# The rows of cumulated step logarithms spread over the partitions by DMA from DRAM, where selector matmuls spread them

## The chip, the cores and the metric

One core of a Trainium2 chip runs the whole program. Five engines work side by side: TensorE (PE, with PEld for its weight loads), VectorE (DVE), ScalarE (ACT), GpSimd (POOL) and SyncE (SP), which here issues most DMAs. Each engine executes its own instructions in the order in which they stand in its queue, and an instruction that must wait for another engine or for a DMA holds up all that stand behind it. The metric is the device time of one execution in microseconds (us). Below, a wide matmul is one of 512 columns with rounded 4-byte operands (lines 141 to 143).

## What is computed

A trunk of two layers over 512 tokens of width 1024. Each layer adds three branches to the stream (differential attention, latent attention, a state-space scan), then a gated feed-forward part. The change lies in the scan. Its core in the reference:

```python
da = (dt * a)                       # 512 tokens x 16 heads, in 4 chunks of 128 tokens
cs = jnp.cumsum(da, axis=2)         # within a chunk
seg = cs[:, :, :, None] - cs[:, :, None, :]
decay = jnp.exp(jnp.where(causal, seg, -jnp.inf))
cb = jnp.einsum('bclgn,bcsgn->bclsg', cm, bm)
y_diag = jnp.einsum('bclsgr,bcsgrp->bclgrp', cb[..., None] * decay, xdt)
```

For each head the kernel needs a matrix exp(min(cs[l], cs[s]) - cs[s]) with s on the partitions and l along the row. So the head's row cs[0..511] has to stand on all 128 partitions.

## The kernel before

Activations lie transposed, features on partitions and the 512 tokens along the row. A product with a weight matrix is taken in three passes, since each operand is split into a rounded part and a rest (hh and hl, wh and wl): `mm3`, lines 140 to 143, for products whose result has features on partitions (`lin_feat`), and lines 220 to 222 for those with tokens on partitions (`lin_tok`). Weights come in pieces of 512 KB by SyncE (tile wr, three buffers); ScalarE makes wh (line 132), VectorE wl (line 133), which frees wr. Products collect in PSUM banks: a pool `mb` of four for the products and a pool `ab` of four for all else.

The scan (in `mix`) runs over four groups of four heads. For group g it takes in text order: two products for x (`lin_feat`, evacuated by `ev_x`: a convolution on ScalarE and VectorE, tile u, lines 873 to 880), the tail of the group before, two products for B and C (`ev_bc`), in the first group `decays`, a product for z (`lin_tok`, evacuated by `ev_z`, tile sz, lines 901 and 902), transposes (lines 910, 922), the products of C and B (line 927, masked into cb, line 929), x scaled by dt (xdt, line 914) and by the decay to the chunk's end (xte, line 934), chunk states (matmuls of line 940, prev, lines 942 to 947), then for each of its four heads r:

- line 953: a matmul whose stationary operand is a column of sel spread over 128 columns, and whose moving operand is cs_r. Rows 0 to 15 of cs_r hold the 16 rounded rows, rows 32 to 47 the rests, all others zero, so the head's row appears on all partitions of a PSUM bank, `ab`;
- line 955: VectorE takes the minimum with the head's column, into tile dec (three buffers);
- line 958: ScalarE, four exponentials in place; line 959: VectorE, dec times cb;
- line 961: eight records of matmuls, dec against xdt, into two banks; after them dec's buffer is free.

Then y collects the two banks (line 964), the read-out of the states (matmuls of line 967, yo and y, lines 969 and 972) and the gate (line 973), its squares go through ScalarE (line 977), the power is taken on GpSimd (line 110, tile yn_r), VectorE scales y (line 982), and the group's tail transposes it on TensorE (line 986) and splits it (lines 989 and 990).

The order of the instructions on each engine isn't written out by hand in this stage: a scheduler lays it out when the program is built, by its own estimates, and mixes the next group's products in between. The buffers of a tile go round in turn, so head n has the dec buffer of head n-3. GpSimd has no DMAs in this stage before the change.

Of the kernel before, what the change touches and what calls it, by code (L numbers as in the profile page):

```python
# [9 lines left out]
F32 = mybir.dt.float32  # L10
F32R = mybir.dt.float32r
I32 = mybir.dt.int32
AF = mybir.ActivationFunctionType
ALU = mybir.AluOpType
# [4 lines left out]
P = 128  # L19
S = 512  # L20
T = S // P
# [8 lines left out]
SSM_H, SSM_G, SSM_HD = 16, 4, 64  # L30
# [35 lines left out]
def trunk_kernel(ctx: ExitStack, tc: tile.TileContext, a: dict, out: bass.AP):  # L66
    nc = tc.nc

    cst = ctx.enter_context(tc.tile_pool(name="cst", bufs=1, reuse_waits="tile"))
# [12 lines left out]
    dram = ctx.enter_context(tc.tile_pool(name="dram", bufs=1, space=DRAM))  # L82
# [4 lines left out]
    def abank():  # L87
        return banks["a"].tile([P, 512], F32, name="ab")
# [5 lines left out]
    ident = cst.tile([P, P], F32, name="ident")  # L94
# [5 lines left out]
    nhalf = cst.tile([P, 1], F32, name="nhalf")  # L100
    nc.vector.memset(nhalf, -0.5)

    sel = cst.tile([P, SSM_H], F32R, name="sel")
    nc.vector.tensor_copy(out=sel, in_=ident[:, 0:SSM_H])
    nc.vector.tensor_copy(out=sel[32:48], in_=ident[0:SSM_H, 0:SSM_H])
    def rstd_of(ss, n, width, name):
        ms = small([P, n], name + "_ms")
        nc.vector.tensor_scalar(out=ms, in0=ss, scalar1=1.0 / width, scalar2=EPS, op0=ALU.mult, op1=ALU.add)
# [464 lines left out]

    bias_d = dram.tile([DA_H, P, BLK[T]], F32, name="bias_d")
    x_d = dram.tile([P, KT, S], F32, name="x_d")
    QG = P // BUCKETS
    NJ = P // (DA_H * QG)
    NSIGN = 5
    early, ahead, SLOW, DEEP = [], [0], (6,), 1
    ORDER = (7, 4, 0, 5, 1, 2, 3, 6)  # L580

    W = 2 * P + QG

# [158 lines left out]
    def mix(l, x, hh, hl, ckr, cq, latp, scope):  # L742
# [93 lines left out]
        nc.vector.scalar_tensor_tensor(out=dt, in0=dt, scalar=0.0, in1=poly, op0=ALU.max, op1=ALU.add)  # L836
        da = ssd.tile([P, T, SSM_H], F32, name="da")
        nc.vector.tensor_tensor(out=da, in0=dt, in1=rv["a"].unsqueeze(1).broadcast_to([P, T, SSM_H]), op=ALU.mult)
        zeros = ssd.tile([P, S], F32, name="cb")
        nc.vector.memset(zeros, 0.0)  # L840
        cs_r = ssd.tile([P, S], F32R, name="cs_r")
        nc.vector.tensor_copy(out=cs_r, in_=zeros)
        cs, ncs, tot, ecs, te = (ssd.tile([P, T, SSM_H], F32, name=nm) for nm in ("cs", "ncs", "tot", "ecs", "te"))

        def decays():

            cp = abank()
            daf = da.rearrange("p t h -> p (t h)")
            nc.tensor.matmul(cp[:, 0:n16], tri, daf, start=True, stop=True)
            nc.tensor.matmul(cp[:, n16:2 * n16], ones, daf, start=True, stop=True)  # L850
            ct = abank()
            for c in range(T):
                nc.tensor.matmul(ct[0:SSM_H, c * P:(c + 1) * P], da[:, c], tri, start=True, stop=True)
            nc.scalar.activation(cs_r[0:SSM_H], ct[0:SSM_H], AF.Copy)
            nc.vector.tensor_tensor(out=cs_r[32:32 + SSM_H], in0=ct[0:SSM_H], in1=cs_r[0:SSM_H], op=ALU.subtract)
            flat = "p t h -> p (t h)"
            nc.vector.tensor_copy(out=cs.rearrange(flat), in_=cp[:, 0:n16])
            nc.vector.tensor_scalar(out=ncs.rearrange(flat), in0=cp[:, 0:n16], scalar1=-1.0, scalar2=None, op0=ALU.mult)
            nc.scalar.activation(ecs.rearrange(flat), cp[:, 0:n16], AF.Exp)
            nc.vector.tensor_tensor(out=te.rearrange(flat), in0=ncs.rearrange(flat), in1=cp[:, n16:2 * n16], op=ALU.add)  # L860
            nc.scalar.activation(te, te, AF.Exp)
            nc.scalar.activation(tot.rearrange(flat), cp[:, n16:2 * n16], AF.Exp)
# [3 lines left out]
        with ssd_scope:  # L866
            tails = []
            for g in range(SSM_G):
# [38 lines left out]
                for i in range(2):  # L907
                    tp = abank()
                    for c in range(T):
# [5 lines left out]
                                            in1=dt[:, :, hs].unsqueeze(3).broadcast_to([P, T, 2, SSM_HD]), op=ALU.mult)  # L915
                    nc.vector.tensor_tensor(out=y[:, :, sl].rearrange("p c (r d) -> p c r d", r=2), in0=tv,
                                            in1=rv["dvec"][:, hs].unsqueeze(1).unsqueeze(3).broadcast_to([P, T, 2, SSM_HD]),
                                            op=ALU.mult)
# [6 lines left out]
                for c in range(T):  # L925
                    cs_ = slice(c * P, (c + 1) * P)
                    nc.tensor.matmul(cbp[:, cs_], bmT[:, cs_], cmT[:, cs_], start=True, stop=True)
                cb = sp.tile([P, S], F32, name="cb")
                nc.vector.tensor_tensor(out=cb.rearrange("p (c l) -> p c l", c=T), in0=cbp.rearrange("p (c l) -> p c l", c=T),
                                        in1=tri.unsqueeze(1).broadcast_to([P, T, P]), op=ALU.mult)  # L930

                xte = sp.tile([P, T - 1, 256], F32, name="xte")
                for c in range(T - 1):
                    nc.vector.tensor_tensor(out=xte[:, c].rearrange("p (r d) -> p r d", r=4),
                                            in0=xdt[:, c].rearrange("p (r d) -> p r d", r=4),
# [13 lines left out]
                yps = [abank().rearrange("p (c d) -> p c d", c=2) for _ in range(2)]  # L949
                for r in range(4):  # L950
                    h = 4 * g + r
                    lp_ = abank()
                    nc.tensor.matmul(lp_, sel[:, h:h + 1].broadcast_to([P, P]), cs_r, start=True, stop=True)
                    dec = sp.tile([P, T, P], F32, name="dec", bufs=3)
                    nc.vector.tensor_tensor(out=dec, in0=lp_.rearrange("p (c l) -> p c l", c=T),
                                            in1=cs[:, :, h:h + 1].broadcast_to([P, T, P]), op=ALU.min)
                    for c in range(T):
                        nc.scalar.activation(dec[:, c], dec[:, c], AF.Exp, bias=ncs[:, c, h:h + 1])
                    nc.vector.tensor_tensor(out=dec, in0=dec, in1=cb.rearrange("p (c d) -> p c d", c=T), op=ALU.mult)
                    for c in range(T):  # L960
                        nc.tensor.matmul(yps[c // 2][:, c % 2, r * SSM_HD:(r + 1) * SSM_HD], dec[:, c],  # L961
                                         xdt[:, c, r * SSM_HD:(r + 1) * SSM_HD], start=True, stop=True)
# [618 lines left out]
```

## Time and profile before

| | |
|---|---|
| median of 3 runs | 2087.01 us (2086.53 to 2087.76) |
| the profiled execution | 2087.19 us |
| its span in the trace | 2085.2 us |
| instructions in the trace | 30158 |
| moved by DMA | 237.20 MB, a mean of 114 GB/s |
| of it by SyncE's queue | 232.63 MB |
| of it by GpSimd's queue | 2.65 MB |

Span and execution differ by 2.0 us at the program's ends. The scan of the first layer lies between 84 and 300 us of the span, that of the second between 1095 and 1310 us. PE is counted busy while a matmul is under way, and the ends of matmuls are modelled, so a busy PE need not be a PE at its peak; idle time on another engine costs nothing while PE has work.

### The profile page before, as it was taken

To read this page: it belongs to the slowest core of one execution; us is meant where nothing else is said; L and a number is where in the kernel's file an instruction comes from. 1 tells how busy PE (TensorE), PEld (TensorE's weight loads), DVE (VectorE), ACT (ScalarE), POOL (GpSimd) and SP (SyncE) were. 2 spreads that over 40 slices of the span, in tenths; PEclk is the share of its full clock that TensorE was granted. 3 is DMA by queue.
4 is the path that set the end of the run, shared out by engine and by line. 5 is a ranking of instruction groups with operands and counts; after the bars stand their busy time and mean duration, and the time that the engine had idled before them with its cause. 6 is when DMAs were issued, how large, how long until landed. Compare 5 with 4: busy or idle time off the path is not lost.

```text
span 2085.2 us, 30158 instructions
## 1 busy us (share of the span) xinstructions
PE 2060.7 (99%) x11469; PEld 1794.4 (86%) x11469; DVE 1415.1 (68%) x2731; ACT 923.4 (44%) x1702; POOL 136.0 (7%) x162
## 2 busy tenths in 40 slices
PE   8999999999999999999999999999999999999999
PEld 7889988899888988888898888889998888888888
DVE  7788887747876778657767887765566566553553
ACT  6744445535533444224344544454444334432431
POOL 4200011002100000000000000110020000000000
PEclk8999999999999999999999999999999999999999
DMA  8523232243455265655443222212333242323322
GB/s 268 154 61 92 71 117 86 86 123 105 143 157 171 85 189 171 193 175 159 156 136 91 71 61 88 64 48 79 95 89 93 91 132 91 101 91 96 97 91 81
DMA packets 224542, 237.20 MB, mean 114 GB/s; under 512 B 16126, under 2 KB 195742, under 8 KB 224142
## 3 DMA queue, kind: packets, MB, share of 16 engines
q1 hardware_dynamic: 221646, 232.63, 36.5%
q0 software_dynamic: 2752, 2.65, 0.5%
q8 instruction: 90, 1.47, 0.3%
q14 instruction: 54, 0.44, 0.1%
HBM read 226.30 MB, written 8.91 MB: 113 GB/s over the span
## 4 chain that ended last, share of the span: by engine, by line
PE 85%; DVE 5%; issue 5%; DMA 2%; POOL 1%; ACT 1%; SPq 0%; POOLq 0%; DVEq 0%; ACTq 0%
PE mb L141 20%; PE mb L142 20%; PE mb L143 20%; PE mb L220 3%; PE mb L222 3%; PE mb L221 3%; PE ab L1168 2%; PE mb L662 1%; PE ab L1136 1%; DMA wg<-in_ada_w_dram 1%; DVE wl L133 1%; PE ab L961 1%; DVE macc L518 1%; PE ab L1319 1%; PE ab L1078 1%
## 5 line engine op out<-in xcount | busy, mean ns | idle before, releaser
L141 PE MATMUL mb<-hh,wh 128*128 128x512 f32 (+1 forms) x1376 | 538.5, 392 | 2.9 <-DVE modsum L530 1.4
L143 PE MATMUL mb<-hh,wl 128*128 128x512 f32 (+1 forms) x1376 | 532.9, 387 | 0.0
L142 PE MATMUL mb<-hl,wh 128*128 128x512 f32 (+1 forms) x1376 | 532.5, 387 | 0.0
L133 DVE TENSOR_TENSOR wl<-wr,wh 128x1024 fp32r<-128x1024 f32 (+2 forms) x312 | 375.2, 1204 | 201.2 <-ACT wh L132 195.5
L132 ACT ACTIVATE wh<-wr 128x1024 fp32r<-128x1024 f32 (+2 forms) x312 | 324.5, 1041 | 337.3 <-PE mb L142 257.4
L141 PEld LDWEIGHTS mb<-hh,wh 128*128 128x128 f32 x1376 | 258.6, 188 | 53.4 <-DVE modsum L530 2.6
L143 PEld LDWEIGHTS mb<-hh,wl 128*128 128x128 f32 x1376 | 258.7, 188 | 51.4
L142 PEld LDWEIGHTS mb<-hl,wh 128*128 128x128 f32 x1376 | 259.0, 188 | 49.0 <-DVE hl L698 1.2
L1416 DVE SCALAR_TENSOR_TENSOR fu<-mb,vec,fu 128x510 f32<-128x510 f32 (+1 forms) x176 | 129.9, 746 | 91.2 <-ACT fu L1414 89.6
L220 PE MATMUL mb<-wh,hh 128*128 128x256 f32 x640 | 182.4, 285 | 0.0
L221 PE MATMUL mb<-wl,hh 128*128 128x256 f32 x640 | 181.2, 283 | 0.0
L222 PE MATMUL mb<-wh,hl 128*128 128x256 f32 x640 | 181.2, 283 | 0.0
L141 PE MATMUL mb<-gh,wh 128*128 128x512 f32 (+1 forms) x432 | 152.3, 353 | 0.0
L143 PE MATMUL mb<-gh,wl 128*128 128x512 f32 (+1 forms) x432 | 151.7, 351 | 0.0
L142 PE MATMUL mb<-gl,wh 128*128 128x512 f32 (+1 forms) x432 | 151.7, 351 | 0.0
L1414 ACT ACTIVATE fu<-mb,vec 128x512 f32<-128x512 f32 x88 | 67.7, 772 | 149.0 <-PE mb L143 149.0
L220 PEld LDWEIGHTS mb<-wh,hh 128*128 128x128 f32 x640 | 122.6, 192 | 0.8 <-ACT wh L132 0.4
L221 PEld LDWEIGHTS mb<-wl,hh 128*128 128x128 f32 x640 | 122.6, 192 | 0.4
L222 PEld LDWEIGHTS mb<-wh,hl 128*128 128x128 f32 x640 | 122.6, 192 | 0.0
L518 DVE SCALAR_TENSOR_TENSOR macc<-wg,c_act,macc 128x512 f32<-128x512 f32 x140 | 104.8, 749 | 22.9 <-DMA wg<-in_ada_w_dram 22.3
L141 PE MATMUL mb<-yh,wh 128*128 128x512 f32 x256 | 105.4, 412 | 0.9 <-ACT g L765 0.9
L142 PE MATMUL mb<-yl,wh 128*128 128x512 f32 x256 | 101.2, 395 | 0.0
(334 smaller groups left out, 3427.4 us busy)
## 6 DMA issues: line engine op xcount, KB each, us to landing
wr<-in_w_in_dram SPq DMA_DIRECT2D x88, 512.0 KB
wr<-in_ffn_w_up_dram SPq DMA_DIRECT2D x88, 512.0 KB
wg<-in_ada_w_dram SPq DMA_DIRECT2D x160, 256.0 KB
wr<-in_ffn_w_down_dram SPq DMA_DIRECT2D x40, 512.0 KB
wr<-in_w_in_dram SPq DMA_DIRECT2D x64, 256.0 KB
wm<-in_ada_w_dram SPq DMA_DIRECT2D x16, 512.0 KB
wr<-in_w_branch_c_dram SPq DMA_DIRECT2D x16, 512.0 KB
wr<-in_w_out_dram SPq DMA_DIRECT2D x16, 512.0 KB
```

Of the source, the lines that this page charges most:

```text
L132: nc.scalar.activation(hi[:, sl], raw[:, sl], AF.Copy)
L133: nc.vector.tensor_tensor(out=lo[:, sl], in0=raw[:, sl], in1=hi[:, sl], op=ALU.subtract)
L141: nc.tensor.matmul(o, lh, rh, start=first, stop=False)
L142: nc.tensor.matmul(o, lh, rl, start=False, stop=False)
L143: nc.tensor.matmul(o, ll, rh, start=False, stop=last)
L220: nc.tensor.matmul(o, hh[:, kk, ts_], wh[:, sl], start=first and k == 0, stop=False)
L221: nc.tensor.matmul(o, hh[:, kk, ts_], wl[:, sl], start=False, stop=False)
L222: nc.tensor.matmul(o, hl[:, kk, ts_], wh[:, sl], start=False, stop=last and k == 3)
L518: ins = nc.vector.scalar_tensor_tensor(out=acc[0], in0=rk, scalar=c_act[:, kk:kk + 1], in1=acc[0], op0=ALU.mult, op1=ALU.add)
L1168: nc.tensor.matmul(po[:, t * P:n], vv[:, j], st["pT"][:, j * P:(j + 1) * P], start=j == 0, stop=j == t)
L1414: nc.scalar.activation(u, bank, AF.Identity, bias=v[:, V_FCB + ti:V_FCB + ti + 1], scale=tap(2))
L1416: nc.vector.scalar_tensor_tensor(out=u[:, s_:], in0=bank[:, 0:S - s_], scalar=tap(2 - s_), in1=u[:, s_:], op0=ALU.mult, op1=ALU.add)
```

## The change

A tensor cs_d of 16 x 512 elements in DRAM takes the place of sel and of the two-part cs_r. `decays` copies the 16 cumulated rows out of PSUM unrounded and GpSimd's queue writes them to cs_d. For each head GpSimd's queue then reads the row into all 128 partitions of the dec tile (256 KB in SBUF), and the minimum is taken in place. The matmul of line 953 and its PSUM bank go, with the setting up of sel (twice 16 columns at the program's start) and of cs_r (a fill, a cast and a subtraction in each layer).

```diff
-    sel = cst.tile([P, SSM_H], F32R, name="sel")
-    nc.vector.tensor_copy(out=sel, in_=ident[:, 0:SSM_H])
-    nc.vector.tensor_copy(out=sel[32:48], in_=ident[0:SSM_H, 0:SSM_H])
...
+    cs_d = dram.tile([SSM_H, S], F32, name="cs_d")
...
-        zeros = ssd.tile([P, S], F32, name="cb")
-        nc.vector.memset(zeros, 0.0)
-        cs_r = ssd.tile([P, S], F32R, name="cs_r")
-        nc.vector.tensor_copy(out=cs_r, in_=zeros)
+        cs_r = ssd.tile([SSM_H, S], F32, name="cs_r")
...
-            nc.scalar.activation(cs_r[0:SSM_H], ct[0:SSM_H], AF.Copy)
-            nc.vector.tensor_tensor(out=cs_r[32:32 + SSM_H], in0=ct[0:SSM_H], in1=cs_r[0:SSM_H], op=ALU.subtract)
+            nc.scalar.activation(cs_r, ct[0:SSM_H], AF.Copy)
+            nc.gpsimd.dma_start(out=cs_d, in_=cs_r)
...
-                    lp_ = abank()
-                    nc.tensor.matmul(lp_, sel[:, h:h + 1].broadcast_to([P, P]), cs_r, start=True, stop=True)
                     dec = sp.tile([P, T, P], F32, name="dec", bufs=3)
-                    nc.vector.tensor_tensor(out=dec, in0=lp_.rearrange("p (c l) -> p c l", c=T),
+                    nc.gpsimd.dma_start(out=dec.rearrange("p c l -> p (c l)"), in_=cs_d[h:h + 1].broadcast_to([P, S]))
+                    nc.vector.tensor_tensor(out=dec, in0=dec,
                                             in1=cs[:, :, h:h + 1].broadcast_to([P, T, P]), op=ALU.min)
```

The scheduler lays the stage out anew. Three places show it. Buffer numbers are kept in the names where they tell heads apart; in the changed kernel line numbers are 3 to 6 lower, so its lines 935, 949, 953, 955, 961 and 976 are 940, 955, 959, 961, 967 and 982 of before.

**TensorE, second head group of the first layer**, from the chunk states on. Before (dec_2113, 2126, 2139, 2152 are the group's four heads; wide matmuls are left out but where one separates two heads):

```order
L940 MATMUL ab_2105<-xte_2093,bmt_2080 128x256
L953 MATMUL ab_2111<-cs_r_1321,sel_86 128x512
...
L961 MATMUL ab_2110<-xdt_2064,dec_2113 128x64 x2
L953 MATMUL ab_2124<-cs_r_1321,sel_86 128x512
L953 MATMUL ab_2137<-cs_r_1321,sel_86 128x512
...
L953 MATMUL ab_2150<-cs_r_1321,sel_86 128x512
...
L961 MATMUL ab_2110<-xdt_2064,dec_2126 128x64 x2
...
L961 MATMUL ab_2110<-xdt_2064,dec_2139 128x64 x2
...
L961 MATMUL ab_2110<-xdt_2064,dec_2152 128x64 x2
```

After (dec_2102, 2114, 2126 and 2138 are the four heads):

```order
L935 MATMUL ab_2096<-xte_2084,bmt_2071 128x256
L955 MATMUL ab_2100<-xdt_2055,dec_2102 128x64 x2
L955 MATMUL ab_2101<-xdt_2055,dec_2102 128x64 x2
L139 MATMUL mb_2187<-hl_945,wh_2183 128x512
L955 MATMUL ab_2100<-xdt_2055,dec_2114 128x64 x2
...
L140 MATMUL mb_2187<-hh_944,wl_2184 128x512
L955 MATMUL ab_2100<-xdt_2055,dec_2126 128x64 x2
...
L138 MATMUL mb_2187<-hh_944,wh_2215 128x512
L955 MATMUL ab_2100<-xdt_2055,dec_2138 128x64 x2
```

Before, 14 wide matmuls stand between the states and the first head's products, and then 10, 2 and 2 before those of the second, third and fourth head. After, the first head follows the states at once, the second and third after one wide matmul each (and one read-out), the fourth after 16 wide matmuls and two read-outs. In the last group of a layer it is 15. The first transposes of the group's tail (line 986) stand 42 wide matmuls behind the fourth head before and 44 after.

**VectorE and GpSimd, the same group.** VectorE before:

```order
L133 TENSOR_TENSOR wl_2331<-wr_2327,wh_2330 128x1024
L955 TENSOR_TENSOR dec_2126<-ab_2124,cs_1323 128x512
L955 TENSOR_TENSOR dec_2139<-ab_2137,cs_1323 128x512
L955 TENSOR_TENSOR dec_2152<-ab_2150,cs_1323 128x512
L959 TENSOR_TENSOR dec_2126<-dec_2126,cb_2091 128x512
...
L959 TENSOR_TENSOR dec_2152<-dec_2152,cb_2091 128x512
L964 TENSOR_TENSOR y_2065<-y_2065,ab_2109 128x512
```

VectorE after (2523, 2535 and 2547 are the first three heads of the next group):

```order
L949 TENSOR_TENSOR dec_2138<-dec_2138,cs_1318 128x512
L963 TENSOR_TENSOR yo_2159<-ab_2157,ecs_1321 128x256
L949 TENSOR_TENSOR dec_2523<-dec_2523,cs_1318 128x512
L949 TENSOR_TENSOR dec_2535<-dec_2535,cs_1318 128x512
L953 TENSOR_TENSOR dec_2138<-dec_2138,cb_2082 128x512
...
L958 TENSOR_TENSOR y_2056<-y_2056,ab_2101 128x512
...
L949 TENSOR_TENSOR dec_2547<-dec_2547,cs_1318 128x512
L966 TENSOR_TENSOR y_2056<-y_2056,yo_2164 128x256
L967 SCALAR_TENSOR_TENSOR y_2056<-y_2056,sz_1940 128x1024
```

GpSimd after (before, its queue has only the yn_r of each group here):

```order
L948 DMA dec_2138<-cs_d_95 128x512
L948 DMA dec_2523<-cs_d_95 128x512
L948 DMA dec_2535<-cs_d_95 128x512
L948 DMA dec_2547<-cs_d_95 128x512
L107 TENSOR_TENSOR yn_r_2179<-yn_ms_2177,nhalf_84 128x4
```

The minima of the next group's first three heads have moved up into this group: two of them stand between the fourth head's minimum and its product with cb, the third between the collecting of y and its gate.

**VectorE, first head group of the first layer**, where the two parts of cs_r were ready. Before:

```order
L880 SCALAR_TENSOR_TENSOR cv_1483<-cv_1483,u_1478 128x512
L860 TENSOR_TENSOR te_1327<-ncs_1324,ab_1486 128x64
L133 TENSOR_TENSOR wl_1804<-wr_1801,wh_1803 128x1024
L902 SCALAR_TENSOR_TENSOR sz_1502<-sz_1502,mb_1509 128x512
L914 TENSOR_TENSOR xdt_1617<-ab_1619,dt_1291 128x4x128
```

After:

```order
L875 SCALAR_TENSOR_TENSOR cv_1478<-cv_1478,u_1473 128x512
L949 TENSOR_TENSOR dec_1659<-dec_1659,cs_1318 128x512
L130 TENSOR_TENSOR wl_1795<-wr_1792,wh_1794 128x1024
L949 TENSOR_TENSOR dec_1671<-dec_1671,cs_1318 128x512
L949 TENSOR_TENSOR dec_1683<-dec_1683,cs_1318 128x512
L897 SCALAR_TENSOR_TENSOR sz_1497<-sz_1497,mb_1504 128x512
L909 TENSOR_TENSOR xdt_1612<-ab_1614,dt_1289 128x4x128
```

The first three minima have moved ahead of the evacuation of z and of xdt. ScalarE's queue has their exponentials in the same way: those of the first head ahead of its first step on z, those of the second and third ahead of its second.

## Rows read from the trace of the kernel before

**Rows 1.** The first part of the page: busy time, share of the span and number of instructions of each engine.

```profile
PE 2060.7 (99%) x11469; PEld 1794.4 (86%) x11469; DVE 1415.1 (68%) x2731; ACT 923.4 (44%) x1702; POOL 136.0 (7%) x162
```

**Rows 2.** The waits of TensorE in the stretch from 84 to 300 us, the whole state-space stage of the first layer: engine, line and tile that waited, on whom, then us in total, times, longest us. It is the only row of the answer; the same question for 1095 to 1300 us, the stage of the second layer, is answered by the same one row.

```profile
PE ab L986 <- DVE y L982: 0.9, 1, 0.9
```

**Rows 3.** Windows of 20 us within the state-space stage of the first layer: length, then busy time (and instructions) of PE, PEld, DVE, ACT and POOL, the granted clock of TensorE, the DMA share, GB/s.

```profile
170.00:190.00 20.00, 20.00 (x116) 17.59 (x115) 16.24 (x29) 8.65 (x22) 0.00 (x0) 1.00 0.19 53
190.00:210.00 20.00, 20.00 (x126) 17.91 (x125) 18.91 (x30) 11.75 (x22) 1.38 (x1) 1.00 0.30 80
```

**Rows 4.** Line 953, the selector matmul, over the whole program: count, ns min/median/max, first and last start in us, forms.

```profile
L953 PE MATMUL ab<-cs_r,sel x32: 391/436/587, 131.3 to 1281.3; 128*128 128x512 f32 x32
```

**Rows 5.** Timeline of TensorE around the second head group of the first layer: start us, us, line, tile, form, count. A logical matmul of 4-byte floats that are not the rounded kind (L961, L967, L940) shows as two records. Matmuls overlap by their modelled ends, so what one costs is read from its start to the next start.

```profile
171.93 0.48 PE L141 MATMUL mb<-hh,wh 128*128 128x512 f32 x1
172.24 0.40 PE L142 MATMUL mb<-hl,wh 128*128 128x512 f32 x1
...
174.98 1.46 PE L940 MATMUL ab<-xte,bmt 128*128 128x256 f32 x6
176.09 0.59 PE L953 MATMUL ab<-cs_r,sel 128*128 128x512 f32 x1
176.51 0.39 PE L142 MATMUL mb<-hl,wh 128*128 128x512 f32 x1
...
179.69 1.00 PE L961 MATMUL ab<-xdt,dec 128*128 128x64 f32 x8
180.50 0.70 PE L953 MATMUL ab<-cs_r,sel 128*128 128x512 f32 x2
181.04 0.39 PE L141 MATMUL mb<-hh,wh 128*128 128x512 f32 x1
...
183.10 0.59 PE L967 MATMUL ab<-prev,cv 128*128 128x256 f32 x2
183.35 0.58 PE L143 MATMUL mb<-hh,wl 128*128 128x512 f32 x1
183.77 0.59 PE L967 MATMUL ab<-prev,cv 128*128 128x256 f32 x2
...
198.04 0.38 PE L986 MATMUL ab<-ident,y 128*128 128x128 f32 x2
```

**Rows 6.** The DMAs that the GpSimd queue issues before the change: their issue on POOL, from the answer on the tile bias_d (count, ns min/median/max), the time from issue to landing of all sixteen, and from the list of DMA issues the smallest ones, with KB each and the median us to landing.

```profile
L666 POOL DMA_DIRECT2D bias_d<-ob x16: 688/735/935, 18.6 to 70.7; - x16
...
DMA to landing us min/median/max: 3.9/5.8/15.7
...
bias_d<-ob POOLq DMA_DIRECT2D x4, 64.0 KB, 5.4
```

**Rows 7.** Timeline of all engines at the start of the program: the one load before the change that has the form of the new ones, a row of 512 elements in DRAM read by all 128 partitions.

```profile
1.26 0.37 SPq L587 DMA_DIRECT2D pk_i<-in_positions_dram  x1
...
5.40 0.43 DVE L610 CAST pk<-pk_i 128x512 f32<-128x512 int32 x1 [3.36 <-DMA pk_i<-in_positions_dram]
```

**Rows 8.** Timelines of SyncE's queue and of GpSimd in the second layer's attention: the loads of the bias rows bt of one head, 64, 128, 192 and 256 KB in this order (L1287), and the GpSimd instructions that wait for each of them (L1288).

```profile
1555.59 0.34 SPq L1287 DMA_DIRECT2D bt<-bias_d  x1
...
1579.60 0.37 SPq L123 DMA_DIRECT2D wr<-in_w_in_dram  x1
1580.63 0.34 SPq L1287 DMA_DIRECT2D bt<-bias_d  x1
...
1557.60 0.29 POOL L1288 TENSOR_SCALAR_AFFINE_SELECT bt<-bt 128x128 f32<-128x128 f32 x1 [0.91 <-DMA bt<-bias_d]
...
1584.65 0.29 POOL L1288 TENSOR_SCALAR_AFFINE_SELECT bt<-bt 128x128 f32<-128x128 f32 x1 [11.00 <-DMA bt<-bias_d]
```

**Rows 9.** Timeline of VectorE in the second head group of the first layer (in square brackets the idle time before, and its releaser).

```profile
173.55 0.68 DVE L929 TENSOR_TENSOR cb<-ab,tri 128x512 f32<-128x512 f32 x1
174.15 1.09 DVE L934 TENSOR_TENSOR xte<-xdt,te 128x256 f32<-128x256 f32 x3
...
192.06 1.22 DVE L973 SCALAR_TENSOR_TENSOR y<-y,sz 128x1024 f32<-128x1024 f32 x1
193.19 1.40 DVE L875 SCALAR_TENSOR_TENSOR u<-mb,vec,u 128x509 f32<-128x509 f32 x2
194.51 1.22 DVE L133 TENSOR_TENSOR wl<-wr,wh 128x1024 fp32r<-128x1024 f32 x1
```

**Rows 10.** Timeline of ScalarE in the second head group of the first layer: the four exponentials of its first head.

```profile
177.44 1.28 ACT L958 ACTIVATE dec<-dec,ncs 128x128 f32<-128x128 f32 x4 [1.45 <-DVE dec L955]
```

**Rows 11.** Groups of instructions of GpSimd: the power that ends the normalisation of a head group; count, busy us, mean ns.

```profile
L110 POOL TENSOR_TENSOR yn_r<-yn_ms,nhalf 128x4 f32<-128x4 f32 x8 | 9.5, 1193 | 367.4 <-DVE yn_ms L108 367.4
```

**Rows 12.** The answer on the tile cs_r: the copy of the cumulated rows out of PSUM, once for each layer.

```profile
L854 ACT ACTIVATE cs_r<-ab x2: 570/570/570, 113.8 to 1125.7; 16x512 fp32r<-16x512 f32 x2
```

**Rows 13.** The first head group of the first layer: timelines of ScalarE, of VectorE and of TensorE, in this order.

```profile
125.28 0.60 ACT L901 ACTIVATE sz<-mb 128x512 f32<-128x512 f32 x1 [2.28 <-PE mb L222]
...
119.28 0.69 DVE L880 SCALAR_TENSOR_TENSOR cv<-cv,u 128x512 f32<-128x512 f32 x1
...
125.72 0.69 DVE L914 TENSOR_TENSOR xdt<-ab,dt 128x512 f32<-128x512 f32 x1 [2.00 <-PE ab L910]
126.33 0.68 DVE L902 SCALAR_TENSOR_TENSOR sz<-sz,mb 128x512 f32<-128x512 f32 x1
...
130.15 1.46 PE L940 MATMUL ab<-xte,bmt 128*128 128x256 f32 x6
```

## The prediction

> **What bounds the kernel now.** I read the busy shares first, then TensorE's waits in the stage that is changed, then the timelines of one head group. TensorE is busy for 99% of the span [rows 1], which by itself says little, as ends are modelled. The waits say more: in the whole scan of a layer it waits 0.9 us once, and the same in the other layer [rows 2]. In the windows of the stage it is busy without a gap at a granted clock of 1.00, while VectorE is at 16.2 to 18.9 of 20 us [rows 3]. So TensorE sets the end here: a matmul removed is a gain, and any wait that the change brings to TensorE is paid in full, because nothing behind it has slack to give back. VectorE is next, with some 10 to 20% to spare, and it holds the evacuations, the weight splits and the minima in one queue.
>
> **What the change removes.** 32 selector matmuls [rows 4]. What one costs is the distance to the next start: in the second group 0.42 us for the first, 0.54 for the next two together, and about 0.27 for the last by the same rate, 1.2 us a group [rows 5]. Eight groups (four in each of two layers): 9.6 us, all on the path. The fill, cast and subtraction of cs_r and the casts of sel are on VectorE away from any wait of TensorE: nothing. The minimum costs VectorE the same from SBUF as from PSUM, since the product with cb, from SBUF, moves as fast as the steps that read PSUM: I take 0.65 us for either, start to result of the next, from the spacing 0.60 at cb [rows 9].
>
> **What it adds.** 32 loads and 2 stores on GpSimd's queue. GpSimd is free (7%) [rows 1], so its issue time matters only as part of a delay. Call L the time from the start of a load's issue to the moment at which VectorE may start on the data. No row shows L itself. The nearest has its form exactly, one row of 2 KB read by 128 partitions, 256 KB, on SyncE's queue: issued at 1.26, used at 5.40, that is 4.1 us [rows 7]. GpSimd's issue takes 0.74 us against 0.37 there [rows 6, 7], so I take **L = 4.5**. Ends: a plain load of 64 KB was used 2.0 us after its issue, one of 256 KB, behind a weight piece, 4.0 us [rows 8]; with the 0.4 for the issue and no queue before it, some 2.6 us is the least I can argue. On the other side the sixteen stores of GpSimd landed after 5.8 us in the median [rows 6]; weight pieces of 512 KB run in this stage too, so 5.8 is my upper end. A load can't bring a gain below these.
>
> The Trainium skill, DMA: Bandwidth & Descriptors, section "Anatomy of one DMA — SWDGE (gpsimd) path", states for a DMA issued by GpSimd a fixed cost of about 2.0 us and the bytes at 436 GB/s besides. By it L would be an estimated 2.6 us and the sum would be the first rival's, below. The load of 64 KB agrees with it, the row of the same form, 4.1 us, doesn't [rows 7, 8].
>
> **Where the loads meet TensorE: the fourth head.** dec has three buffers, so heads one to three of a group can be loaded long before, and the fourth only when the first head's matmuls are done. I walk the second group in the new order with the durations of before. 13 wide matmuls and the states end at 176.09 [rows 5]. VectorE has xte done at 175.2 [rows 9] and the first product with cb 0.6 later, in time, and so are the next two. A head's eight records take 0.81, a wide matmul after them 0.31, a read-out with the next wide matmul 0.67 [rows 5]: the first head ends at 176.9, the second at 178.0, the third at 179.5. One wide matmul (0.31), two read-outs (0.5), a wide one (0.42) and 14 more at 0.228 (13 take from 171.93 to 174.98) lead to the fourth head, due at 183.9.
>
> Its own load starts at 177.0. But in VectorE's new order the minima of two heads of the next group stand ahead of its product with cb, and the second of these is loaded into the third head's buffer, from 179.6 on. So the product is done at 179.6 + L + 0.65 + 0.65, and with 0.1 for the hand-over the fourth head starts at 181.0 + L. The stall is L - 2.9: **1.6 us**. ScalarE's four exponentials of the fourth head, 1.28 us [rows 10], fit in between. Behind the waiting VectorE stand a weight split and the adds to y, behind TensorE everything.
>
> **The tail.** The third of the next group's early loads goes into the fourth head's buffer, from 184.8 + stall on; its minimum stands on VectorE ahead of the last add to y and the gate, and behind it come four steps of the convolution and then the small step ahead of the power. From its end, 185.5 + stall + L: 0.4 for the add, 1.13 for the gate, 4 x 0.66 for the steps [rows 9], 0.1, 1.2 for the power [rows 11], 0.3 and 0.1 for scaling and hand-over, 5.9 in all, so y is ready at 191.4 + stall + L. TensorE comes to the first transposes of the tail 44 wide matmuls after the fourth head, at 194.8 + stall. (Before, they came at 198.04 [rows 5], without a wait.) This second stall is L - 3.4, **1.1 us**, and some 0.4 for the other six transposes, whose scalings come after one more step.
>
> So each group that has a successor changes by -1.2 + 1.6 + 1.5 = +1.9 us; six such groups: +11.4. The last group of a layer has no successor's minima: there the fourth head waits only for its own chain, 177.0 + L + 0.65 + 1.28 + 0.65 + 0.2 = 179.8 + L against 183.7 (15 wide matmuls), a stall of 0.6, and -0.6 in all; twice: -1.2.
>
> **The start of the stage.** cs_r leaves PSUM at 113.8 + 0.57 [rows 12]; the store to DRAM starts at 114.5. Stores of GpSimd landed after 3.9 us at the least, the 64 KB ones after 5.4 in the median [rows 6]; this one has 32 KB, I take 4.6 and keep both. The first row is then there at T = 114.5 + 4.6 + 0.1 + 4.5 = 123.7. VectorE waits for it from 119.9 (0.6 after 119.28), with the split, z and xdt queued behind (before, it did them at 125.72 [rows 13], after idling 2.0 us). What ends last goes through ScalarE: 0.65 for the minimum, 1.3 exponentials, 0.6 for the first step on z, 2.6 for the next two heads' exponentials, 0.6 for the second step on z [rows 10, 13], then VectorE's step on it 0.6, four steps at 0.6 and the first xte 0.4: T + 9.2 = 132.9. The states were due at 130.15 [rows 13]: a stall of **2.75 us**. The other layer has the same distances (cs_r at 1125.7 [rows 12]), so 5.5.
>
> **Sum.** 11.4 - 1.2 + 5.5 = +15.7 us on the profiled execution's 2087.19, which is its span and 2.0 us around it; the changed parts all lie in the span. That makes 2102.9; the median of the runs is 0.2 lower: **2102.7**.
>
> **Rivals.** All hang on L.
> 1. *The loads are quick, and the matmuls' time stays saved.* At L = 2.6 neither the fourth head (L - 2.9) nor the tail (L - 3.4) waits, and with the fastest store, 3.9, the start stalls 3.9 + 2.6 - 6.35, or 0.15 us a layer. Sum: -9.6 + 0.3 = -9.3, so 2077.7. For it: the 64 KB load at 2.0 us, and the stage's DMA share of 0.19 to 0.30 [rows 3, 8]. Against: the row of the same form at 4.1 [rows 7]. The place is the fourth head of every group; from L = 3.3 downward the kernel is faster by over 0.2%. It is also where the rule of the Trainium skill above leads.
> 2. *Gain and stalls cancel.* At L = 3.6, store 3.9: six times -1.2 + 0.7 + 0.6, twice -1.2, twice 1.15: +0.5, so 2087.5 for the median of the runs. From L = 3.3 to 3.85 the sum stays within 4.2 us.
> 3. *The loads are slow.* At L = 5.8 and a store of 5.4: six times -1.2 + 2.9 + 2.8, twice -1.2 + 1.9, twice 4.85: +38.1, so 2125.3. For it: the stores' median [rows 6], and weight pieces of twice the size on the same DMA engines. Against: those stores went to DRAM, in the program's busiest stretch.
>
> **How the numbers follow.** A measurement of this kernel can tell about 0.2%, 4.2 us, from no change. L between 3.85 and 5.2 (my forecast): 0.46, 2091 to 2115. Above that: 0.18. Between 3.3 and 3.85: 0.14. Below: 0.22. So slower 0.64, same 0.14, faster 0.22. The range runs from L = 2.9 (-8, a tenth below it) to L = 5.5 (+33, a tenth above): 2079 to 2121. The forecast's own range is 2091 to 2115.
>
> **What would show it.** Right: TensorE has waits in each group, for the fourth head's dec (about 1.6 us, not in the last group) and at the tail's transposes for y (about 1.1), and in the first group of each layer one for xte (about 2.75); VectorE waits for DMAs into dec before the minima of the fourth head and of the next group's; GpSimd's loads land some 4 us after their issue. Wrong: TensorE's waits stay at 0.9 us a layer, and the stage shortens by 1.2 us a group; or the landing is under 3 us, or over 5.5. It would also be wrong if VectorE's waits push the weight splits behind TensorE's needs, a term that I set at zero because each piece is split well before its product starts.

## The result, and the profile after

| | before | after |
|---|---|---|
| device time, median | 2087.39 us (2086.53 to 2088.62, 4 runs) | 2105.11 us (2103.3 to 2108.11, 4 runs) |
| profiled execution, span | 2085.2 us | 2101.6 us |
| busy: TensorE, VectorE, GpSimd | 2060.7, 1415.1, 136.0 us | 2060.1, 1411.3, 156.6 us |

The ratio is 1.0081, with a 95% interval of 1.0069 to 1.0094: slower by 0.8%. Forecast: 2102.7.

**Where TensorE waits now.** The two largest waits of TensorE over the whole execution (for what; us in all, times, the longest). Lines of the changed kernel are 3 to 6 lower: L955 is a head's product, L980 the tail's transpose.

```profile
PE ab L955 <- DVE dec L953: 11.5, 6, 2.1
PE ab L980 <- DVE y L976: 5.3, 5, 1.8
```

The first row is new: six waits, as many as there are groups with a successor. The second was 0.9 us in each layer before [rows 2], and those two waits, in the last groups, are still among the five. No row names xte (L935): at the start of the stage nothing waits.

The timeline of TensorE in the second group (start, duration, engine, line; in brackets the idle time ahead and what ended it), which answers to [rows 5]:

```profile
171.78 1.03 PE L905 MATMUL ab<-ident,cv 128*128 128x128 f32 x8
...
181.64 0.48 PE L138 MATMUL mb<-hh,wh 128*128 128x512 f32 x1
...
186.02 0.39 PE L138 MATMUL mb<-hh,wh 128*128 128x512 f32 x1
188.51 1.56 PE L955 MATMUL ab<-xdt,dec 128*128 128x64 f32 x8 [2.10 <-DVE dec L953]
189.83 0.77 PE L139 MATMUL mb<-hl,wh 128*128 128x512 f32 x1
190.40 0.63 PE L140 MATMUL mb<-hh,wl 128*128 128x512 f32 x1
190.83 0.63 PE L138 MATMUL mb<-hh,wh 128*128 128x512 f32 x1
...
192.11 0.53 PE L138 MATMUL mb<-hh,wh 128*128 128x512 f32 x1
192.48 0.39 PE L139 MATMUL mb<-hl,wh 128*128 128x512 f32 x1
...
201.23 0.41 PE L980 MATMUL ab<-ident,y 128*128 128x128 f32 x2
```

Two things are to be seen. TensorE idles 2.10 us ahead of the fourth head. And then it runs slowly: the head's eight records take 1.32 us to the next start (0.81 before [rows 5]), and wide matmuls start 0.43 apart until 192.48, where they go back to 0.23. That is the lower of the clock's two levels, 1.2 GHz in place of 2.4. The stretch from 188.51 to 192.48 takes 3.97 us; in the second layer's second group, where the clock stays up after such a wait, the same records take 2.38:

```profile
1209.88 1.10 PE L955 MATMUL ab<-xdt,dec 128*128 128x64 f32 x8 [1.94 <-DVE dec L953]
...
1212.26 0.39 PE L139 MATMUL mb<-hl,wh 128*128 128x512 f32 x1
```

So **1.6 us** are lost after the wait. The windows of the first layer say the same in the column of the granted clock (start and end; length; busy time of PE, PEld, DVE, ACT, POOL; granted clock; DMA share; GB/s):

```profile
184.00:204.00 20.00, 17.90 (x79) 14.38 (x78) 15.16 (x28) 13.09 (x33) 1.58 (x2) 0.91 0.26 78
204.00:224.00 20.00, 20.00 (x144) 18.89 (x144) 16.06 (x25) 7.27 (x11) 0.00 (x0) 1.00 0.39 106
```

**Why the fourth head is late.** GpSimd's timeline and VectorE's over the same stretch. The load at 179.67 is the fourth head's; those at 180.80, 182.35 and 190.37 are the next group's first three.

```profile
179.67 0.60 POOL L948 DMA_DIRECT2D dec<-cs_d  x1 [28.00 <-DVE prev L942]
180.80 0.54 POOL L948 DMA_DIRECT2D dec<-cs_d  x1 [0.53 <-PE ab L961]
182.35 0.54 POOL L948 DMA_DIRECT2D dec<-cs_d  x1 [1.02 <-PE mb L138]
190.37 0.54 POOL L948 DMA_DIRECT2D dec<-cs_d  x1 [7.47 <-DVE y L958]
```

```profile
183.35 0.69 DVE L949 TENSOR_TENSOR dec<-dec,cs 128x512 f32<-128x512 f32 x1 [0.67 <-DMA dec<-cs_d]
...
184.43 0.69 DVE L949 TENSOR_TENSOR dec<-dec,cs 128x512 f32<-128x512 f32 x1
187.16 0.69 DVE L949 TENSOR_TENSOR dec<-dec,cs 128x512 f32<-128x512 f32 x1 [2.03 <-DMA dec<-cs_d]
187.77 0.69 DVE L953 TENSOR_TENSOR dec<-dec,cb 128x512 f32<-128x512 f32 x1
...
194.52 0.69 DVE L949 TENSOR_TENSOR dec<-dec,cs 128x512 f32<-128x512 f32 x1 [2.72 <-DMA dec<-cs_d]
195.13 0.42 DVE L966 TENSOR_TENSOR y<-y,yo 128x256 f32<-128x256 f32 x1
195.58 1.23 DVE L967 SCALAR_TENSOR_TENSOR y<-y,sz 128x1024 f32<-128x1024 f32 x1
```

The fourth head's own row was there at 183.35, 3.68 us after its issue. Its product with cb, at 187.77, stands behind two minima of the next group, and the second of these waited 2.03 us for a load issued at 182.35: 4.81 us from issue to use. The last add to y and the gate stand in the same way behind the minimum at 194.52 (4.15 us from its issue).

The load that counts is also a slow one. SyncE issues a weight piece 0.4 us behind it:

```profile
182.75 0.37 SPq L201 DMA_DIRECT2D wr<-in_w_in_dram  x1
```

In the packets of the trace, 16 of the 32 loads overlap with no weight piece and land after 3.3 to 3.9 us; 14 overlap with 325 KB or more of one and land after 4.1 to 4.8, among them, in all six groups, the load in question (4.4 to 4.8). The second profile of this kernel (e9, below) shows the same, with 4.4 to 4.6 for the load in question. No run moves the weight pieces away, so that the cause is not shown.

Time from issue to landing: of all loads (least, median, most), then by transfer (count, size, median):

```profile
DMA to landing us min/median/max: 3.3/3.8/4.8
```

```profile
dec<-cs_d POOLq DMA_DIRECT2D x32, 256.0 KB, 3.8
...
cs_d<-cs_r POOLq DMA_DIRECT2D x2, 32.0 KB, 1.9
```

**Where the 16.4 us of the span lie.** The start of a group's transposes (L910 before, L905 after) divides the stage; the last figure of a layer is from there to its last tail.

| distance, us | first layer | second layer |
|---|---|---|
| before | 44.83, 43.52, 43.52, 27.09 | 44.83, 43.54, 43.52, 27.10 |
| after | 48.34, 46.75, 46.70, 24.64 | 47.95, 46.29, 46.16, 24.48 |

Six groups with a successor: +18.4 us. The two last groups: -5.1, but in the new order their tail stands 8 wide matmuls earlier (458 of them between 84 us and the last tail of the first layer before, 450 after), 8 x 0.228 = 1.82 us in each, and these come back behind it; that leaves -1.4. The rest of the program: -0.6.

### The profile page after: what moved, and what is told of

It is laid out like the page before. It is cut to its first block, busy times and chain, and to the rows that moved or that the text cites. A ratio compares the mean times of both kernels' runs of the same rounds, so it can differ in the third digit from the quotient of the medians.

```text
span 2101.6 us, 30227 instructions
## 1 busy us (share of the span) xinstructions
PE 2060.1 (98%) x11437; PEld 1786.7 (85%) x11437; DVE 1411.3 (67%) x2722; ACT 920.5 (44%) x1703; POOL 156.6 (7%) x196
## 4 chain that ended last, share of the span: by engine, by line
PE 84%; DVE 6%; DMA 5%; issue 3%; ACT 1%; POOL 1%; SPq 0%; DVEq 0%; POOLq 0%; ACTq 0%
PE mb L138 20%; PE mb L139 20%; PE mb L140 20%; PE mb L217 3%; PE mb L219 3%; PE mb L218 3%; DMA dec<-cs_d 2%; PE ab L1162 2%; PE ab L1130 1%; DMA wg<-in_ada_w_dram 1%; PE ab L955 1%; DVE wl L130 1%; DVE macc L515 1%; PE ab L1313 1%; PE ab L1072 1%
## 5 line engine op out<-in xcount | busy, mean ns | idle before, releaser
L140 PE MATMUL mb<-yh,wl 128*128 128x512 f32 x256 | 101.1, 395 | 0.0
```

Of the source, the lines that this page charges most:

```text
L140: nc.tensor.matmul(o, ll, rh, start=False, stop=last)
```

## The experiments

Theory 1: TensorE's wait for the fourth head, with what follows from it (the lower clock, the wait for y), is the whole loss. Theory 2: the loads themselves cost the time. Theory 3: the removed matmuls were worth nothing.

**Four buffers (e1_dec4).**

```
-        cs_r = ssd.tile([SSM_H, S], F32, name="cs_r")
+        cs_r = ssd.tile([P, S], F32, name="cb")[0:SSM_H]
-                    dec = sp.tile([P, T, P], F32, name="dec", bufs=3)
+                    dec = sp.tile([P, T, P], F32, name="dec", bufs=4)
```

> The changed kernel with four buffers for dec instead of three (the cumulated logarithms are put into a tile that is free at that time, to make room). The load of the fourth head then has a buffer long before the first head's matmuls. Theory 1 (TensorE waits for the fourth head's load, loses more to the lower clock that follows the wait, and waits again for y): the waits before the heads' matmuls fall from 11.5 us to under 3 us, the granted clock stays at 1.00 in all windows of the scan, and what is left is the removed selector matmuls: 2078 to 2084 us, faster than both kernels. Theory 2 (the loads themselves, 256 KB each beside the weights' pieces, cost the time): as many loads as before, so about 2105 us.

Measured: 2079.26 us (2077.66 to 2081.85), 0.9955 of the kernel before, interval 0.9941 to 0.9969. TensorE waits for no head, and for y 0.6 us in all. The scan's window of the first layer, columns as above:

```profile
84.00:300.00 216.00, 215.35 (x1263) 190.59 (x1261) 172.16 (x330) 102.53 (x230) 21.13 (x27) 0.99 0.38 108
```

The same 32 loads land (108 GB/s where the kernel before moves 88 in this window), and TensorE loses nothing to them. (The clock's missing hundredth lies ahead of the first group, from 84 to 104 us.) In this kernel's order the next group's minima stand behind y's gate. Groups two and three take 42.6 us against 43.5 before; the first groups gain less (44.4 and 44.8, 44.8 before). Theory 2 is out. It beats both kernels.

**No loads (e2_noload).**

```
-                    nc.gpsimd.dma_start(out=dec.rearrange("p c l -> p (c l)"), in_=cs_d[h:h + 1].broadcast_to([P, S]))
-                    nc.vector.tensor_tensor(out=dec, in0=dec,
+                    nc.vector.tensor_tensor(out=dec, in0=ones.unsqueeze(1).broadcast_to([P, T, P]),
```

> The changed kernel without the 32 loads: the minimum is taken against ones in place of the heads' rows, so the rows' part of the computation is left out; the two stores stay. A floor for the change. Theory 1 and theory 2: no wait for a load and no traffic, 2087.4 - 9.6 = about 2078 us. Theory 3 (the selector matmuls lay in time that TensorE loses anyway, so that the gain of 1.2 us a group doesn't exist): about 2087 us, and then the loads cost 18 us in all instead of 27.

Measured: 2081.99 us, ratio 0.9968 (0.9956 to 0.9981). Groups two and three take 42.60, 0.92 less than before, so theory 3 is out; the total is 4 us above what was expected, of which 2.8 are waits for y, as the tail's transposes stand earlier in this order. A kernel with its loads (e1) is not slower than one without, though their orders differ.

**Loads that nothing reads (e3_idle_load).**

```
...
+                    row = sp.tile([P, T, P], F32, name="row")
+                    nc.gpsimd.dma_start(out=row.rearrange("p c l -> p (c l)"), in_=cs_d[h:h + 1].broadcast_to([P, S]))
...
-                    nc.vector.tensor_tensor(out=dec, in0=dec,
+                    nc.vector.tensor_tensor(out=dec, in0=ones.unsqueeze(1).broadcast_to([P, T, P]),
```

> The changed kernel with its 32 loads going into a tile of one buffer that nothing reads; the minimum is taken against ones, so the rows' part of the computation is left out. All the traffic and all of GpSimd's issues, but no engine waits for them. Theory 1 (waits): the same as without loads within 3 us, 2077 to 2081 us. Theory 2 (traffic): 2100 to 2106 us.

Measured: 2110.41 us, ratio 1.0104 (1.009 to 1.0118). Neither theory expected this: by theory 1 it should have been quick, and the time is above theory 2's. The experiment was badly built. With one buffer each load waits for the one before it, in GpSimd's queue, and the power for y's norm (yn_r) stands in that queue behind eleven of them. GpSimd's timeline, then TensorE's waits:

```profile
150.21 0.54 POOL L948 DMA_DIRECT2D row<-cs_d  x1 [3.38 <-DMA row<-cs_d]
154.06 0.54 POOL L948 DMA_DIRECT2D row<-cs_d  x1 [3.31 <-DMA row<-cs_d]
157.88 0.54 POOL L948 DMA_DIRECT2D row<-cs_d  x1 [3.29 <-DMA row<-cs_d]
158.43 1.03 POOL L107 TENSOR_TENSOR yn_r<-yn_ms,nhalf 128x4 f32<-128x4 f32 x1
```

```profile
PE ab L981 <- DVE y L977: 27.8, 4, 13.1
```

Two waits of 13.1 and 12.6 us, in the first group of each layer, make up 25.8 of the 28.4 us by which it stands above e2; groups two and three take 42.60, but all loads of the layer are done by then, so that this run does not test theory 2. It is an in-order queue again.

**The fourth head alone undone (e4_hybrid),** with sel and cs_r as before beside the store.

```
...
+                    if r == 3:
+                        lp_ = abank()
+                        nc.tensor.matmul(lp_, sel[:, h:h + 1].broadcast_to([P, P]), cs_r, start=True, stop=True)
...
+                    if r < 3:
+                        nc.gpsimd.dma_start(out=dec.rearrange("p c l -> p (c l)"), in_=cs_d[h:h + 1].broadcast_to([P, S]))
...
```

> The changed kernel with the fourth head of each group undone alone: its row is spread by a selector matmul as in the kernel before, the other three heads' rows come by DMA. Theory 1: no wait for the fourth head's load and no fall of the clock after it; three quarters of the removed matmuls stay removed (-7 us); the third early load of the next group still waits for the fourth head's matmuls, so up to 1.5 us a group at y may stay in six groups: 2080 to 2089 us. Theory 2: three quarters of the loads, so about 2100 us.

Measured: 2082.26 us, ratio 0.9974 (0.9963 to 0.9985), 42.87 for groups two and three. No wait before a head; 0.8 us in all for y. With 24 of the 32 loads it keeps 0.65 us a group of the gain. Theory 1 holds.

**The next group's loads held back (e5_late_next).** What makes the fourth head late, its own load or the order on VectorE?

```
+                    if g and r < 3:
+                        nc.vector.tensor_copy(out=dec[0:1, 0, 0:1], in_=cv[0][0:1, 0:1])
                     nc.gpsimd.dma_start(out=dec.rearrange("p c l -> p (c l)"), in_=cs_d[h:h + 1].broadcast_to([P, S]))
```

> The changed kernel with three buffers as it is, but the loads of the next group's first three heads can't start before the next group's first convolved tile is there: one element of it is copied into dec before each of these loads, 18 tiny copies on VectorE. The fourth head's own load starts when it did. Theory 1a (the fourth head waits because the minima of two heads of the next group, and so their loads, stand ahead of its product on VectorE): the wait before the fourth head falls from 1.9 us to under 0.5, the wait for y to under 0.5, the clock stays at 1.00: 2079 to 2084 us. Theory 1b (its own load, which has to wait for the first head's matmuls, is simply too late): 1.5 to 2 us of wait stay in each of six groups, with the lower clock after them: 2096 to 2103 us.

Measured: 2083.5 us, ratio 0.9985 (0.9976 to 0.9994). TensorE's waits in the stage of the first layer, then VectorE's rows of the second group's fourth head:

```profile
PE ab L982 <- DVE y L978: 1.4, 2, 0.9
PE ab L957 <- DVE dec L955: 0.5, 1, 0.5
```

```profile
180.85 0.69 DVE L951 TENSOR_TENSOR dec<-dec,cs 128x512 f32<-128x512 f32 x1 [0.56 <-DMA dec<-cs_d]
...
183.03 0.69 DVE L955 TENSOR_TENSOR dec<-dec,cb 128x512 f32<-128x512 f32 x1 [1.15 <-ACT dec L954]
```

Now 2.2 us lie between the fourth head's minimum and its product (the exponentials), where the changed kernel has 4.4. One wait of 0.5 us before a head is left in the whole program, the clock stays up, and of the waits for y only those of the last groups (0.9, as before the change) are over 0.5. Three buffers are enough, and the fourth head's load, which still waits for the first head's matmuls, is in time: theory 1a.

**A tile of its own for the rows (e6_row1).**

```
...
+                    row = sp.tile([P, T, P], F32, name="row")
+                    nc.gpsimd.dma_start(out=row.rearrange("p c l -> p (c l)"), in_=cs_d[h:h + 1].broadcast_to([P, S]))
                     dec = sp.tile([P, T, P], F32, name="dec", bufs=3)
...
+                    nc.vector.tensor_tensor(out=dec, in0=row,
```

> The changed kernel with the rows loaded into a tile of their own (one buffer), from which the minimum writes into dec (three buffers); the cumulated logarithms are put into a tile that is free at that time, to make room. A row's load now waits for the minimum before it, not for a head's matmuls. Theory 1 (the loads' time counts only because a load has to wait for matmuls): under 3 us of waits before the heads in all, 2078 to 2085 us. Theory 2 (the loads themselves): about 2105 us.

Measured: 2091.16 us, ratio 1.0021 (1.0012 to 1.003), 6 us above the expected range. No head waits, as theory 1 has it, and groups two and three take 42.65 to 43.05. The first group of each layer takes 48.1 and 49.3 (44.8 before): there nothing could be loaded ahead, and with one buffer a row's load waits for the minimum before it. TensorE's waits for xte in both layers, then VectorE's for the rows in the first:

```profile
PE ab L935 <- DVE xte L929: 3.5, 2, 1.8
```

```profile
DVE dec L950 <- DMA row<-cs_d: 10.2, 7, 2.2
```

The wait for xte is the one that the prediction feared for the changed kernel; here, with loads in series, it comes. In the same two groups TensorE waits 2.1 us for VectorE's collecting of y (at L812) and 1.6 before y's transposes; with the 3.5 for xte that is 7.2 us, which is where this kernel loses.

**Selector matmuls doubled (e7_sel2),** on the kernel before.

```
                     nc.tensor.matmul(lp_, sel[:, h:h + 1].broadcast_to([P, P]), cs_r, start=True, stop=True)
+                    nc.tensor.matmul(lp_, sel[:, h:h + 1].broadcast_to([P, P]), cs_r, start=True, stop=True)
```

> The kernel before with each of the 32 selector matmuls issued twice into the same bank. The price of one, alone. If the removed matmuls were worth 1.2 us a group, as the prediction has it: +9.6 us, 2097 us; at the least the issue distance of a wide matmul, 0.228 us each: +7.3, 2094.7 us. Theory 3 (they lay in time that TensorE loses anyway): no change, 2087 us.

Measured: 2095.81 us, ratio 1.0045 (1.0032 to 1.0058), +9.3. Groups two and three take 44.7, 1.2 us more than before. Adding four matmuls costs 1.2 us a group; taking them away (e1, e2) gave 0.92 to 0.95 in the same groups.

**A later first row (e8_hop2).**

```
...
-            nc.gpsimd.dma_start(out=cs_d, in_=cs_r)
+            nc.gpsimd.dma_start(out=cs_e, in_=cs_r)
+            nc.gpsimd.dma_start(out=cs_f, in_=cs_e)
+            nc.gpsimd.dma_start(out=cs_d, in_=cs_f)
```

> The changed kernel with two more copies, DRAM to DRAM, between the store of the cumulated logarithms and the loads of the rows, so that the first row comes later in each layer; all else as it is. It tests the chain at the start of the stage, which showed no wait in the changed kernel. The prediction's chain (T + 9.2 us from the first row's arrival T to the last of the products on which the states wait) leaves 0.35 us to spare there: T is 118.96 and the states are due at 128.51. If that chain holds, two copies at some 2.5 us each (the store's 1.9 and its issue) move T to about 124 and TensorE waits some 4.6 us for xte in each layer: 2114 us, up to 2118 if the clock falls after the waits. If the chain was wrong, and the start has slack: TensorE waits under 2 us in all, 2105 to 2107 us.

Measured: 2101.96 us, ratio 1.0067 (1.0053 to 1.0081), below both expectations. The order changed with the edit: two of the three minima went behind the products on which the states wait. VectorE, then TensorE:

```profile
126.73 0.69 DVE L953 TENSOR_TENSOR dec<-dec,cs 128x512 f32<-128x512 f32 x1 [3.61 <-DMA dec<-cs_d]
...
130.93 1.09 DVE L933 TENSOR_TENSOR xte<-xdt,te 128x256 f32<-128x256 f32 x3
```

```profile
131.49 1.53 PE L939 MATMUL ab<-xte,bmt 128*128 128x256 f32 x6 [1.33 <-DVE xte L933]
```

So the chain of T + 9.2 was not tested: here it is 4.2 from T to the first xte, with a wait of 1.3 and 1.7 us in the two layers. And the first groups have no wait before a head (four in all, 8.0 us, instead of six), which makes up for it. Inconclusive for the chain.

**The changed kernel again (e9_after_again).** No edit.

> The changed kernel unchanged, profiled once more, for the clock alone. In the first profile the lower clock followed four of the six waits before a fourth head (waits of 1.7 to 2.1 us). If the fall hangs on the place in the program, the same four places show it again; if it hangs on how a wait falls in time, other places or another number of them do. The waits themselves should be the same within 0.2 us, and where the clock doesn't fall, the wait for y should be about 1.3 us longer. Time about 2105 us in either case.

Measured: 2106.08 us. Six waits before a head, 11.2 us in all. The lower clock followed four of them again, but not the same four: in the first layer's third group it stayed away, where the first profile has it, and in the second layer's second group it came, where the first profile has none (in that layer's first group it came too, and in its third it stayed away). So it does not hang on the place alone. TensorE in the first two:

```profile
236.33 1.10 PE L955 MATMUL ab<-xdt,dec 128*128 128x64 f32 x8 [1.93 <-DVE dec L953]
...
248.94 0.41 PE L980 MATMUL ab<-ident,y 128*128 128x128 f32 x2 [1.44 <-DVE y L976]
```

```profile
1213.22 1.11 PE L955 MATMUL ab<-xdt,dec 128*128 128x64 f32 x8 [1.82 <-DVE dec L953]
...
1214.98 0.63 PE L139 MATMUL mb<-hl,wh 128*128 128x512 f32 x1
```

Where the clock stays up, the tail waits for y by 1.0 to 1.8 us (four such groups in the two profiles); where it falls, by 0 to 0.5 (eight).

## Why the prediction came out as it did

The forecast's case came: the fourth head's wait turns a saving of matmuls into a loss. The sum was +15.7, the span grew by 16.4, but the terms did not all hold: that the total came so near is luck, as two errors offset each other.

- **The gain**, 1.2 us a group: doubling shows that price exactly (e7), removal gave 0.92 to 0.95 in groups two and three (e1, e2), less in the first groups of e1. Too large by a quarter; where that quarter went is open. The minimum from SBUF, taken at 0.65 from a row that reads PSUM [rows 9], takes 0.61 (187.16 to 187.77).
- **L**, taken as 4.5: 3.48 at the start of the first layer, and in the second group 3.68, 4.81 and 4.15. The 4.5 fits the loads that count (4.4 to 4.8 to their landing), but those beside no weight piece land after 3.3 to 3.9: the prediction got to 4.5 from a row at the program's start and GpSimd's longer issue, and named the weight pieces only for its upper end and its third rival. With an L of 3.8 its own formula gives a wait of 0.9. The rule in the Trainium skill, DMA: Bandwidth & Descriptors, section "Anatomy of one DMA — SWDGE (gpsimd) path", would give an estimated 2.6 us for these loads and 2.1 for the store of 32 KB: the store agrees (1.9), the loads don't (3.3 at the least). The measurements decide.
- **The fourth head**, 1.6 us: the waits are 1.74 to 2.10, 11.5 us in six. The mechanism is shown, down to the row: with L = 4.81 for the load that counts, the formula L - 2.9 gives 1.9. e5 takes away what stands ahead on VectorE, and the wait is gone. The last groups have no such wait. The signs in the prediction say so, its sum has 0.6 us in each; their fourth load lands 3.6 and 3.7 us after its issue, under the L of 3.9 from which the sum would have them wait. They save 1.4 together, and 1.2 was predicted.
- **The tail**, 1.5 us (1.1 at the first transposes, 0.4 at the others): near where the clock stays at its full level. There the first transposes wait 1.77 and 1.28 (1.44 and 1.02 in e9), and the others show no wait. In the second layer's second group, whose fourth head waits 1.94:

```profile
1222.32 0.41 PE L980 MATMUL ab<-ident,y 128*128 128x128 f32 x2 [1.28 <-DVE y L976]
```

  In four of six groups the clock's fall, which no step foresaw, makes TensorE late by 1.6 us, y is then ready when it comes, and the tail's wait shrinks to 0.4 or nothing. The one takes the other's place, so that a group is 46.3 us without the fall and 46.2 to 46.8 with it (groups two and three). Together, six groups lose 18.4 instead of 11.4: -5.6 for the matmuls, 11.5 before the heads, 3.4 for y, 6.4 for four falls of the clock, and 2.7 that are left. Most of these, by an estimate from the second group, lie around the waits: the profile counts a wait from the modelled end of the matmul before it, while from start to start (186.02 to 188.51, less 0.23) it is 2.26 and not 2.10, and a head's records after a wait take 0.91 and not 0.81 at the full clock (1209.88 to 1210.79).
- **The start of the stage**, 5.5 us: this step failed. Its chain began at T = 123.7 on the time axis of before, which is 122.1 here, as the stage comes 1.64 earlier. GpSimd's rows, then VectorE's, ScalarE's and TensorE's show T = 118.96 and the states at once:

```profile
113.02 0.57 POOL L850 DMA_DIRECT2D cs_d<-cs_r  x1 [18.51 <-ACT cs_r L849]
115.48 1.65 POOL L948 DMA_DIRECT2D dec<-cs_d  x3 [1.89 <-issue]
```

```profile
118.96 0.69 DVE L949 TENSOR_TENSOR dec<-dec,cs 128x512 f32<-128x512 f32 x1 [1.27 <-DMA dec<-cs_d]
...
124.07 0.69 DVE L909 TENSOR_TENSOR xdt<-ab,dt 128x512 f32<-128x512 f32 x1 [1.49 <-PE ab L905]
```

```profile
123.78 0.58 ACT L896 ACTIVATE sz<-mb 128x512 f32<-128x512 f32 x1
```

```profile
128.50 1.46 PE L935 MATMUL ab<-xte,bmt 128*128 128x256 f32 x6
```

  The loads start 2.5 us after the store, not 4.7, and L is 1.0 shorter there. The store's price was bounded by 3.9 and 5.4 from stores [rows 6] that the same text called those of the busiest stretch; the lower end was no lower end. At 124.07 VectorE even waits 1.49 us for TensorE's transposes. With T as measured, the prediction's own chain leaves no stall: T + 9.2 is 128.16. Its walk behind T is borne out in its first half, where ScalarE's second step on z was to end at T + 5.75 and ends at 124.36, T + 5.4; what a late T would cost no run shows, since e8 changed the order.
- **Weight splits**, set at zero: no row shows TensorE waiting for one in the stage.

So the total was near by luck, as a term of 5.5 that did not come stood against 7 that were missing in the six groups.

## What to carry to other kernels

A transfer that takes the place of a cheap matmul is free only if its result is not in front of other work in an in-order queue: look in the new order for what stands behind the instruction that waits for it, and for which buffer the transfer itself waits. Here a fourth buffer, or an artificial dependence that holds back the next group's loads, turns 0.8% slower into 0.45% or 0.15% faster with the same transfers. And when TensorE is the bound, price an idle gap of 2 us at more than its length (1.6 us more in eight of twelve cases here), unless something later waits anyway. A transfer's time from issue to use should be taken beside the traffic that runs where it counts, not from a quiet stretch.

## What the runs showed of the hardware that was not expected

- After idling 1.7 to 2.1 us in a stretch that was busy throughout, TensorE's granted clock fell to the lower level in eight of twelve cases (two profiles of one kernel); a wide matmul then starts every 0.43 us instead of 0.23, for 4 to 8 of them, and 1.6 us are lost. After waits of the same length it also stayed up (1.94 without, 1.74 with). What decides is open.
- A load by GpSimd of one row of 2 KB to 128 partitions lands after 3.3 to 4.8 us in the changed kernel (median 3.8): 3.3 to 3.9 where no weight piece moves at the same time, 4.1 to 4.8 beside 325 KB or more of one. In e1, where four go in a row, one beside no weight piece took 4.96, and the last of four issued 0.53 us apart while weight pieces move took 5.8 and 6.15. A store of 32 KB to DRAM lands after 1.9.
- Loads into a tile of one buffer that nothing reads still run in series, 3.6 to 5.1 us apart, as the program lets each wait for the one before, and hold up GpSimd's arithmetic behind them (TensorE then waited 13.1 and 12.6 us in e3).
